# Dealing the first 512 rows of x to the first two row pairs in turn, in a fused QKV projection

## The chip, the cores and the metric

The kernel runs on one core of one Trainium2 chip. The metric is the device time of one execution in microseconds (us), as the median of several runs. Before the change it is 358.25 us, the median of 3 runs from 358.24 to 358.67 us.

TensorE (PE in the profile) multiplies, VectorE (DVE), ScalarE (ACT) and GpSimd (POOL) convert, add and copy, and SyncE (SP) issues most of the transfers between DRAM and the core's own memory. A transfer is carried by 16 DMA engines side by side.

## The reference

```python
def setup_inputs():
    batch, seq, hidden = 16, 512, 768
    return {
        "x": np.random.randn(batch, seq, hidden).astype(np.float32),
        "w_qkv": np.random.randn(hidden, 3 * hidden).astype(np.float32),
    }

def reference(x, w_qkv):
    qkv = np.matmul(x, w_qkv)
    q, k, v = qkv[..., :768], qkv[..., 768:1536], qkv[..., 1536:]
    return np.stack([q, k, v], axis=0).astype(np.float32)
```

It is one matrix product, 8192 x 768 by 768 x 2304, whose three column thirds are written as three separate arrays of 8192 x 768. Each row of the output depends on the same row of x alone, so which rows are worked on together is free, as long as a result is written back to the row that it came from.

## The kernel before, in words

The 8192 rows of x are worked on in 32 pairs of row tiles (`NP`), two tiles of 128 rows to a pair. The 2304 output columns are cut into two groups of 1024 (`Q_OFF`, the index `q`), each of two blocks of 512 (`CB`), and a remainder of 256 (`REM`). Pairs 2 to 31 multiply each group by a scheme of seven products for a 2 x 2 block product, which needs sums of blocks of x (`sums_x`) and of w (`sum_w`); products 1 and 2 are in bf16 and the others in f32r, and all go through line 245. Pairs 0 and 1 (`ND = 2`) are multiplied directly in bf16, in `block` (line 479), because the sums of w are not there yet. The remainder columns of every pair are multiplied directly in `rem` (line 308).

The order of the work is written out by hand (`manual_schedule`): each engine runs its instructions in the order in which the program issues them, and waits only for data or for a buffer. The transfers that SP issues are one ordered queue.

The start runs like this. SP first issues the loads of pair 0 and of pair 1 (`load_rows`, line 160), 768 KB each: partition m receives row m of the first tile and row m of the second, two pieces of 3072 bytes. Behind them in the same queue come the first weight block in six loads of 256 KB (`load_blocks(0, 0, 1)`, line 92), the second in two of 768 KB, the remainder's weights, and pair 2 in eight loads (`load_x_rows(2)`, line 137), which reads pieces of 768 bytes. Beside the loads TensorE multiplies zeros (`busy`, line 452). When pair 0 has landed, ACT and DVE convert it to bf16, each a share of the columns (`cast_row`, lines 165 and 166), TensorE turns it (`turn_row`, line 179), and DVE and ACT copy the turned tiles out of PSUM (`copy_row`, lines 186 and 188). Two more products of zeros follow, and then pair 1 goes the same way. After its twelve turns TensorE goes straight on to the products of the first weight block (line 479) and from there to the end of the program.

Results are stored by `store_quad` (two stores of 768 KB and 256 KB for each pair and column group, lines 298 to 303) and, for the remainder, by the last line of `rem` (line 323, 256 KB). For all pairs these take their place in DRAM from `rows_of`. Pairs 0 and 1 have eight stores of the first kind and two of the second. The remainder's staging tile has two buffers (`or_pool`), so the copy of pair 2's remainder out of PSUM (line 322) waits until the store of pair 0's has landed. The output tiles have five buffers (`o_pool`), and the input tiles three (`xin_pool`).

Pair 5 is loaded behind most of the stores of pairs 0 and 1 in SP's queue (`load_x(ND + 3, nc.sync)`, line 128); DVE then turns it (line 153), and POOL makes its sums (lines 212 to 216), which the seven products need.

Of the kernel before, what the change touches and what calls it, by code (L numbers as in the profile page):

```python
# [10 lines left out]
def kernel(  # L11
# [20 lines left out]
    nc = tc.nc  # L32
    P = 128
# [6 lines left out]
    KH = KT // 2  # L40
    KC = K // 4
    NP = M // (2 * P)
    CB = 512
    REM = N3 - 4 * CB
    Q_OFF = (0, 2 * CB + REM)
    R_OFF = 2 * CB
    fp32 = mybir.dt.float32
# [6 lines left out]
    x_flat = x.rearrange("b t h -> (b t) h")  # L54
    out_flat = out.rearrange("s b t h -> s (b t) h")
# [21 lines left out]

    b1 = [w_pool.tile([P, KT, CB], bf16, name=f"b1_{q}") for q in range(2)]
    b22 = [w_pool.tile([P, KH, CB], f32r, name=f"b22_{q}") for q in range(2)]
    t_0 = w_pool.tile([P, 4, KH, CB], f32r, name="t_0")  # L80
    w_rem[1] = rem_pool.tile([P, KH, REM], bf16, name="w_rem1")
# [39 lines left out]
    xin, xf, xb, sr = {}, {}, {}, {}  # L121
# [19 lines left out]
    def load_x(p, other):  # L141
        xin[p] = xin_pool.tile([P, 2 * P // G, KC], fp32, name="xin")
        load_x_half(p, 0, nc.sync)
        if other is not None:
            load_x_half(p, 1, other)

    def transpose(p, cuts=(0, 8)):
        if p not in xf:
            xf[p] = xf_pool.tile([P, KT, 2 * P], fp32, name="xf")
        turned = xf[p][:].rearrange("p j (g b) -> p g j b", b=G)  # L150
        rows = xin[p][:].rearrange("p g (a j) -> p g j a", a=G)
        for g, end in zip(cuts, cuts[1:]):
            nc.vector.transpose(turned[:, g:end], rows[:, g:end])  # L153

    def load_rows(p):
        xin[p] = xin_pool.tile([P, 2, K], fp32, name="xin")
        rows = x_flat[p * 2 * P:(p + 1) * 2 * P, :]
        nc.sync.dma_start(xin[p][:], rows.rearrange("(r m) k -> m r k", m=P))  # L160

    xc, turned_rows = {}, {}

# [63 lines left out]
    def quad(p, q, pool=o_pool, tag="o"):  # L227
        u = Quad()
        u.p, u.q = p, q
        u.o = pool.tile([P, 2, 2 * CB], fp32, name="o", tag=tag)  # L230
        u.x = u.y = u.z = None
        return u

    def product(u, n, ps, start):
        t1, t2, t3, t4 = ts[u.q]
        if n <= 2:
            h = (n - 1) * KH
            lhs = [xb[u.p][:, h + j, :P] for j in range(KH)]
            rhs = [b1[u.q][:, h + j, :] for j in range(KH)]
        else:  # L240
            k, t = {3: (4, b22[u.q][:]), 4: (0, t4), 5: (1, t1), 6: (2, t2), 7: (3, t3)}[n]
            lhs = [sr[u.p][:, k, j, :] for j in range(KH)]
            rhs = [t[:, j, :] for j in range(KH)]
        for j in range(KH):
            nc.tensor.matmul(  # L245
                ps[:], lhs[j], rhs[j],
                start=(start and j == 0), stop=(j == KH - 1), skip_group_check=True,
            )
# [7 lines left out]
    def do(u, n, out=True):  # L256
# [17 lines left out]
        elif n == 5:  # L274
            u.y = bank()
            product(u, 5, u.y, True)
            if u.p == NP - 1:
                nc.scalar.activation(c22, u.y[:], ident)
        elif n == 7:
            product(u, 7, u.x, False)  # L280
            if u.p == NP - 1:
                nc.vector.tensor_tensor(c22, c22, u.x[:], op=add)
# [8 lines left out]
            nc.vector.tensor_tensor(c12, c12, u.y[:], op=add)  # L291

    def rows_of(s, p, lo, hi):
        return out_flat[s, p * 2 * P:(p + 1) * 2 * P, lo:hi].rearrange("(r m) n -> m r n", m=P)

    def store_quad(u):
        if u.q == 0:
            nc.sync.dma_start(rows_of(0, u.p, 0, H), u.o[:, :, :H])
            nc.sync.dma_start(rows_of(1, u.p, 0, 2 * CB - H), u.o[:, :, H:])
        else:  # L300
            part = 2 * H - Q_OFF[1]
            nc.sync.dma_start(rows_of(1, u.p, H - part, H), u.o[:, :, :part])
            nc.sync.dma_start(rows_of(2, u.p, 0, H), u.o[:, :, part:])
# [9 lines left out]
    def rem(p, eng=nc.sync, between=None):  # L313
        ps = ps_pool.tile([P, 2, REM], fp32, name="ps")
        rem_row(p, 0, ps[:, 0, :])
        if between is not None:
            between()
        rem_row(p, 1, ps[:, 1, :])

        def copied():  # L320
            o = or_pool.tile([P, 2, REM], fp32, name="orem")
            act.activation(o[:], ps[:], ident)  # L322
            return lambda: eng.dma_start(rows_of(1, p, R_OFF - H, R_OFF - H + REM), o[:])

        return copied

    def two(a, b, early, u=None):

        do(a, 1)
        do(b, 1, u is None)  # L330
        if u is None:
            early()
            rem(a.p)()()
        else:
            middle(u)
            copied = rem(a.p, between=lambda: third(u))
            evacuate(b)
            early()
            copied()()
            fourth(u)  # L340
            load_x(a.p + 3, nc.sync)
        do(a, 2)
        do(b, 2)
        summed(a, b)
# [27 lines left out]
    def plain(a, b, c, d, early, rem_c, stored=False):  # L372

        add_first(a)
        add_first(b)
        rem(a.p)()()
        do(c, 1)
        do(d, 1)
        early()
        rem_c()  # L380
        do(c, 2)
        do(d, 2)
        add_second(a)
        add_second(b)
        if stored:
            for u in (c, d):
                store_cols(u, 0, 0, CB, nc.sync)
# [43 lines left out]
        rem_stored(a.p, 1, 2, lambda dst, src: act.activation(dst, src, ident), nc.sync)  # L431


    ND = 2
    zero = xb_pool.tile([P, CB], bf16, name="zero", tag="xb")
    nc.vector.memset(zero[:], 0.0)
    load_rows(0)
    nc.scalar.activation(tiny[:], zero[:, :1], ident)
    make_identity(nc, eye)
    load_rows(1)  # L440
    load_blocks(0, 0, 1)
    load_blocks(0, 1)
# [66 lines left out]
    def ahead(p, reversed_pair):  # L509
        transpose(p)  # L510
        if reversed_pair:
            sums_x(p)
            round_x(p)
        else:
            round_x(p)
            sums_x(p)
# [114 lines left out]
    def load_next(p, other):  # L631
        if p < NP:
            load_x(p, other)

    def early():
        ahead(ND + 2, False)
        load_x(ND + 3, nc.sync)

    two(quad(ND + 1, 0), quad(ND + 1, 1), early, u2)

    def early():
        ahead(ND + 3, True)
        load_x(ND + 5, nc.sync)

    two(quad(ND + 2, 0), quad(ND + 2, 1), early)
    transpose(ND + 4, (0, 4))

    for p in range(ND + 3, NP - 1, 2):
        first = p == ND + 3
# [6 lines left out]
        def early():  # L656
            ahead(p + 2, p + 2 < NP - 1)
            load_next(p + 4, nc.scalar)
# [6 lines left out]
        c, d = quad(p + 1, 0), quad(p + 1, 1)  # L665
        final = p + 3 >= NP
        plain(a, b, c, d, early, lambda: rem(c.p)()(), final)
# [32 lines left out]
```

## Time and profile before

| | before |
|---|---|
| median of 3 runs | 358.25 us (358.24 to 358.67) |
| the profiled execution's own time | 358.3 us |
| its span, first to last instruction | 356.5 us |
| TensorE busy | 351.5 us, 99% of the span |
| DVE, ACT, POOL busy | 264.3, 186.0, 177.3 us |
| read from DRAM, written to DRAM | 32.24 MB, 75.50 MB |
| granted TensorE clock, mean | 1.000 |

The profile is of one execution. The difference between its own time and its span, 1.8 us, lies before its first instruction and after its last. A page of the profile gives each engine's busy time, the transfers, and the chain of work that ended last, followed back from the last instruction. Beside it the trace can be asked for who waited for whom, for the chain in order of time, and for the busy time and the bytes moved in any stretch of the span. It also has a record of every packet that a DMA engine moved, with its start, its length in time and its size.

### The profile page before, as it was taken

The numbers are of one execution on the slowest core, as the hardware profiler recorded it, in microseconds if no ns is written. First come the engines' busy times: TensorE is split into PE (matmuls) and PEld (weight loads), VectorE is DVE, ScalarE is ACT, GpSimd is POOL, SyncE is SP. The second block draws the span as 40 slices with busy tenths as digits, with TensorE's granted clock in tenths as the row PEclk, the third lists the DMA queues.
The fourth block names the chain that finished last, engine by engine and source line by source line (L and its number), as shares of the span: only waits on it lengthen the run. The fifth ranks groups of instructions, "written<-read, shape, count | busy, mean of one in ns | idle before, by whom it ended". The sixth has DMA issues, their size and how long they took to land.

```text
span 356.5 us, 5348 instructions
## 1 busy us (share of the span) xinstructions
PE 351.5 (99%) x1782; PEld 252.2 (71%) x1782; DVE 264.3 (74%) x309; ACT 186.0 (52%) x321; POOL 177.3 (50%) x184
## 2 busy tenths in 40 slices
PE   7999999999999999999999999999999999999996
PEld 3474677768677686877768677686877868777675
DVE  3799876796877869777695876969777696876743
ACT  4587755445454553645545454553645545454553
POOL 0121773376566453665535566353665535566320
PEclk9999999999999999999999999999999999999999
DMA  7998999999999898998979889699999989887397
GB/s 297 379 351 258 323 373 344 371 325 360 293 337 311 250 362 204 357 258 299 351 189 385 229 311 338 174 406 242 346 272 299 331 196 390 232 295 293 146 377 273
DMA packets 82075, 108.10 MB, mean 303 GB/s; under 512 B 4992, under 2 KB 62080, under 8 KB 82048
## 3 DMA queue, kind: packets, MB, share of 16 engines
q1 hardware_dynamic: 75520, 103.04, 86.2%
q10 hardware_dynamic: 6528, 4.72, 5.1%
q8 instruction: 14, 0.23, 0.3%
q14 instruction: 13, 0.11, 0.1%
HBM read 32.24 MB, written 75.50 MB: 302 GB/s over the span
## 4 chain that ended last, share of the span: by engine, by line
PE 97%; DMA 2%; ACT 0%; SPq 0%; issue 0%
PE ps L245 79%; PE ps L308 11%; PE ps L479 6%; DMA xin<-in_x_dram 2%; PE ps L412 0%; PE ps L179 0%; ACT xc L166 0%; SPq L160 0%; ACT orem L431 0%
## 5 line engine op out<-in xcount | busy, mean ns | idle before, releaser
L245 PE MATMUL ps<-t,s 128*128 128x512 f32 x720 | 178.0, 395 | 0.0
L245 PEld LDWEIGHTS ps<-t,s 128*128 128x128 f32 x720 | 135.0, 188 | 29.6
L153 DVE STREAM_TRANSPOSE xf<-xin 128x768 f32<-128x768 f32 (+2 forms) x46 | 93.4, 2033 | 2.8 <-DMA xin<-in_x_dram 2.8
L245 PE MATMUL ps<-b,xb 128*128 128x512 bf16 x360 | 85.2, 379 | 0.0
L285 DVE TENSOR_TENSOR o<-o,ps 128x512 f32<-128x512 f32 x56 | 38.5, 687 | 51.8 <-ACT o L284 51.8
L192 POOL CAST xb<-xf 128x1536 bf16<-128x1536 f32 x28 | 41.0, 1465 | 56.9 <-DVE xf L153 56.9
L212 POOL TENSOR_TENSOR s<-xf 128x384 fp32r<-128x384 f32 x29 | 31.0, 1067 | 72.9 <-DVE xf L153 71.2
L245 PEld LDWEIGHTS <-xb 128*128 128x128 bf16 x360 | 34.0, 98 | 36.9 <-issue 4.2
L291 DVE TENSOR_TENSOR o<-o,ps 128x512 f32<-128x512 f32 x60 | 41.1, 686 | 20.7 <-PE ps L245 19.5
L284 ACT ACTIVATE o<-ps 128x512 f32<-128x512 f32 x56 | 33.5, 598 | 42.1 <-PE ps L245 42.1
L245 PE MATMUL ps<-b,s 128*128 128x512 f32 x180 | 50.6, 389 | 0.0
L288 ACT ACTIVATE o<-ps 128x512 f32<-128x512 f32 x60 | 35.9, 598 | 25.2 <-PE ps L245 22.8
L365 DVE TENSOR_TENSOR o<-o,ps 128x512 f32<-128x512 f32 x78 | 47.8, 681 | 0.0
L273 ACT ACTIVATE o<-ps 128x512 f32<-128x512 f32 x60 | 36.0, 599 | 19.1 <-PE ps L245 15.4
L308 PE MATMUL ps<-w_rem,xb 128*128 128x256 bf16 x372 | 45.7, 273 | 0.0
L322 ACT ACTIVATE orem<-ps 128x512 f32<-128x512 f32 x31 | 18.5, 597 | 49.1 <-PE ps L308 28.5
L308 PEld LDWEIGHTS <-xb 128*128 128x128 bf16 x372 | 36.2, 98 | 10.9 <-issue 0.3
L245 PEld LDWEIGHTS ps<-b,s 128*128 128x128 f32 x180 | 33.8, 188 | 7.0
L213 POOL TENSOR_TENSOR s<-s,xf 128x384 fp32r<-128x384 f32 x29 | 29.5, 1018 | 2.3
L214 POOL TENSOR_TENSOR s<-xf 128x384 fp32r<-128x384 f32 x29 | 29.4, 1015 | 0.0
L216 POOL TENSOR_TENSOR s<-xf,s 128x384 fp32r<-128x384 f32 x29 | 29.2, 1008 | 0.0
L369 ACT ACTIVATE o<-ps 128x512 f32<-128x512 f32 x26 | 15.5, 598 | 16.9 <-PE ps L245 16.1
(53 smaller groups left out, 164.9 us busy)
## 6 DMA issues: line engine op xcount, KB each, us to landing
out_dram<-o SPq DMA_DIRECT2D x60, 768.0 KB, 4.7
out_dram<-o SPq DMA_DIRECT2D x76, 256.0 KB, 3.9
xin<-in_x_dram SPq DMA_DIRECT2D x88, 192.0 KB, 5.6
out_dram<-orem SPq DMA_DIRECT2D x31, 256.0 KB, 2.4
xin<-in_x_dram ACTq DMA_DIRECT2D x24, 192.0 KB, 4.4
st<-in_w_qkv_dram SPq DMA_DIRECT2D x5, 768.0 KB, 7.7
xin<-in_x_dram SPq DMA_DIRECT2D x2, 768.0 KB, 4.9
st<-in_w_qkv_dram SPq DMA_DIRECT2D x6, 256.0 KB, 6.0
```

Of the source, the lines that this page charges most:

```text
L153: nc.vector.transpose(turned[:, g:end], rows[:, g:end])
L192: nc.gpsimd.tensor_copy(out=xb[p][:], in_=xf[p][:])
L212: 1: lambda g: g.tensor_tensor(s[:, 1], a21, a22, op=add),
L213: 2: lambda g: g.tensor_tensor(s[:, 2], s[:, 1], a11, op=sub),
L245: nc.tensor.matmul(ps[:], lhs[j], rhs[j], start=(start and j == 0), stop=(j == KH - 1), skip_group_check=True,)
L273: nc.scalar.activation(c12, u.x[:], ident)
L284: nc.scalar.activation(c22, u.x[:], ident)
L285: nc.vector.tensor_tensor(c22, c22, u.y[:], op=add)
L288: nc.scalar.activation(c21, u.x[:], ident)
L291: nc.vector.tensor_tensor(c12, c12, u.y[:], op=add)
L308: nc.tensor.matmul(ps, xb[p][:, j, r * P:(r + 1) * P], w_rem[j // KH][:, j % KH, :], start=(j == 0), stop=(j == KT - 1), skip_group_check= ...
L365: dve.tensor_tensor(c, c, u.z[:], op=add)
```

## The change

The two pairs that are multiplied directly, 0 and 1, take other rows than before. Pair 0 held rows 0 to 255 and pair 1 rows 256 to 511; now pair 0 holds the even and pair 1 the odd rows of the first 512. In each pair, partition m of tile r has row 256 r + 2 m + p instead of row 256 p + 128 r + m. The loads follow this and so do all stores of the two pairs, through `rows_of`. The pieces keep their size (3072 bytes in a load, 3072 or 1024 in a store) and their number. In DRAM two neighbouring partitions of one tile are 6144 bytes apart instead of 3072, and the two rows of one partition 786,432 bytes instead of 393,216. The second argument of `load_rows` has a default that leaves one transfer to a pair, and no call gives another. `ND` is only set earlier.

```diff
+    ND = 2
...
-    def load_rows(p):
+    def dealt(rows, p):
+        return rows[:ND * 2 * P].rearrange("(r m p) n -> p m r n", m=P, p=ND)[p]
+
+    def load_rows(p, tiles=2):
         xin[p] = xin_pool.tile([P, 2, K], fp32, name="xin")
-        rows = x_flat[p * 2 * P:(p + 1) * 2 * P, :]
-        nc.sync.dma_start(xin[p][:], rows.rearrange("(r m) k -> m r k", m=P))
+        for r in range(0, 2, tiles):
+            n = slice(r, r + tiles)
+            nc.sync.dma_start(xin[p][:, n], dealt(x_flat, p)[:, n])
...
     def rows_of(s, p, lo, hi):
+        if p < ND:
+            return dealt(out_flat[s, :, lo:hi], p)
         return out_flat[s, p * 2 * P:(p + 1) * 2 * P, lo:hi].rearrange("(r m) n -> m r n", m=P)
...
-    ND = 2
```

## The prediction

> **What bounds the kernel now.** I read the shares by engine first, then the chain that ended last, then the waits, and last the stretches of the span that the change touches. The table of stretches says how far TensorE leaves room (busy us and instructions of PE, PEld, DVE, ACT, POOL, then clock, DMA share, GB/s):
>
> ```profile
> 0.00:7.44 7.44, 5.39 (x24) 2.22 (x25) 1.82 (x6) 2.98 (x6) 0.70 (x6) 1.00 0.72 276
> 7.44:351.50 344.06, 344.06 (x1738) 248.49 (x1739) 261.36 (x302) 181.89 (x313) 176.63 (x178) 1.00 0.92 304
> ```
>
> From 7.44 to 351.50 us TensorE is never idle. So the end moves only in two ways: the moment 7.44 moves, or a hole opens in those 344 us. The chain in order of time says what sets 7.44:
>
> ```profile
> 0.74 0.44 SPq L160
> 1.24 5.62 DMA xin<-in_x_dram
> 6.88 0.45 ACT xc L166
> 7.44 0.85 PE ps L179 x12
> 8.29 0.86 PE ps L479 x4
> ```
>
> The landing of pair 1's rows at 6.86 starts the conversion, the conversion starts the turns, and after these TensorE does not stop. A microsecond on this landing is a microsecond on the end. Pair 0 is ahead in the same queue, so what matters is when 1.57 MB (two times 768 KB) have arrived. The rate of the transfers by stretch:
>
> ```profile
> 1.90:2.40 0.50, 0.50 (x2) 0.15 (x1) 0.00 (x0) 0.32 (x2) 0.00 (x0) 1.00 0.54 104
> 2.40:2.90 0.50, 0.50 (x3) 0.18 (x2) 0.00 (x0) 0.00 (x0) 0.00 (x0) 1.00 0.79 258
> 2.90:3.40 0.50, 0.50 (x3) 0.23 (x2) 0.00 (x0) 0.00 (x0) 0.00 (x0) 1.00 1.04 424
> 3.40:6.40 3.00, 2.59 (x19) 1.25 (x17) 0.84 (x3) 0.94 (x2) 0.00 (x0) 1.00 1.02 413
> ```
>
> ```profile
> 6.90:10.80 3.90, 3.45 (x26) 1.92 (x26) 3.02 (x9) 3.30 (x9) 0.00 (x0) 1.00 1.05 405
> ```
>
> ```profile
> 17.00:18.00 1.00, 1.00 (x6) 0.46 (x5) 1.00 (x2) 0.21 (x1) 1.00 (x2) 1.00 1.12 241
> ```
>
> ```profile
> 34.00:38.00 4.00, 4.00 (x20) 1.78 (x19) 4.00 (x4) 4.00 (x9) 0.36 (x1) 1.00 1.04 411
> ```
>
> The loads of pairs 0 and 1 ramp up for one microsecond and then run at 413 to 424 GB/s. The packet records show the same: the first one or two packets of 3072 bytes on an engine take 119 to 576 ns, and from 3.0 us to the end of both loads nearly every one takes 121 ns. The last engine's part of pair 1 lands at 6.86, the first one's at 6.34.
>
> **The change part by part.**
>
> *Instructions.* Nothing is added, removed or moved on any engine or queue: two loads and ten stores get other DRAM addresses, with pieces of the same size and number. The moved `ND` and the loop in `load_rows` issue what was issued before: one transfer to a pair. This costs 0, and needs no cover.
>
> *The steady part of the two loads.* It runs at 413 to 424 GB/s with the rows of a tile 3072 bytes apart. The weight loads from 6.90 to 10.80 read 2048-byte pieces that lie 55,296 bytes apart (six rows of w to a partition), nine times the new distance, at 405 GB/s. Both ends of the distance scale run within 5% of each other, and packet times of 121 ns without scatter say that each DMA engine moves at its own pace, not at DRAM's. Lower end: at 424 instead of 413 the steady 3.9 us would shorten by 0.1. Upper end: the slowest stretch of loads in the trace, 241 GB/s at 17 to 18 us, where pair 2 is read in 768-byte pieces from 96 KB of DRAM; 1.57 MB would take 6.5 us there instead of 3.8, 2.7 more. The weight loads are the nearer row, since their pieces are long and spread out as the new ones are. I take 0 and keep -0.1 and +2.7.
>
> *The ramp of the two loads.* From 1.90 to 2.90 us the transfers moved 0.5 x (104 + 258) = 181 KB; at 413 GB/s they would have moved 413. The missing 232 KB are 0.56 us. If the slow first packets come from engines that meet in the same part of DRAM, larger distances could shorten this; if they come from opening more places, they would lengthen it. The trace has another ramp, when the next weight block is read after pair 2 (18.5 to 20 us): there the pieces lie far apart, and single first packets still take 540 to 741 ns. So distance alone does not remove slow first packets, though 768-byte loads are in flight beside them. Lower end: the whole 0.56 us go; if also the spread in the engines' first packets (1.92 to 2.51 us) went, 32 packets of 118 ns each from 1.92 and the 0.30 us from the last packet's end to its landing would give 5.98, 0.88 earlier. Upper end: the ramp doubles, +0.56. I take 0.
>
> *What moves with the landing.* Everything behind the two loads in SP's queue shifts with them, since the engines work the queue off in order: the weight rows land from 7.50 on, and TensorE's start shifts by the same time. So the head is carried over one to one.
>
> *The ten stores.* They carry 4 x 768 + 4 x 256 + 2 x 256 KB = 4.7 MB between 28 and 54 us, and two waits hang on them:
>
> ```profile
> ACT orem L322 <- DMA out_dram<-orem: 1.9, 1, 1.9
> DVE xf L153 <- DMA xin<-in_x_dram: 2.4, 1, 2.4
> ```
>
> The first is the copy of pair 2's remainder, which waits until 31.96 for the store of pair 0's remainder. Behind it on ACT stand the last three conversions of a weight block (line 457), which end at 34.60; TensorE started that block at 32.40 and wants the third of them after 14 products of 0.22 us, at 35.5. The cover is 0.9 us. The second is pair 5's turn, which waits until 56.36 for its load behind the stores; POOL's second sum of it ends at 61.65, and TensorE asks for it at 63.86. The cover is 2.2 us. Bounds: the stores of both shapes ran at 411 GB/s from 34 to 38 us, paced by the engines (121 ns and 46 ns a packet), so a gain buys nothing, TensorE having no hole there to close: 0. At the slow end, 241 instead of 411 GB/s, 4.7 MB would take 19.5 us instead of 11.4, 8 more, of which 5.9 would be left over the cover of 2.2. I take 0, because the stores that are there now include 1024-byte pieces 3072 bytes apart as well as whole rows, and both run at the engines' pace.
>
> *Sum.* 0 + 0 + 0 against the profiled execution's 358.3 us (356.5 span and 1.8 around it). The median of the runs is 358.25, 0.05 below it, so I predict 358.25 us: no change. A difference of less than 0.2%, 0.72 us, is about what a measurement of this kernel can't tell from no change.
>
> **A rule against this change.** The row first: the trace reads at 413 GB/s with 3072 bytes between partitions and at 405 GB/s with 55,296. The Trainium skill, "DMA: Bandwidth & Descriptors", section "Latency and other measured facts", reports that copies slow down when the rows of the partitions lie at large powers of two apart: 207 GB/s at 512 KiB, 164 at 2 MiB, 103 at 4 MiB. Here the distances become 6 KiB between partitions and 768 KiB between a partition's two rows, three times a power of two. By the page's figures I estimate at most a fall as from 207 to 164, to 0.79 of the rate, which would make the 3.8 us of the loads 1.0 longer; by the rows it is 0. No run here has yet shown a rate at these distances.
>
> **The rivals.**
>
> *The ramp gets shorter.* For it: the first packets take up to 576 ns against 121, and the next ones do not. Against it: the other ramp, over far places, has longer ones. Removing 0.28 to 0.56 us gives 357.7 to 358.0; the extreme of 0.88 us gives 357.4. Even that is cut: TensorE's ten products of zeros run until 5.2, and turning pair 0 and two more products of zeros need 1.4 us after that, so pair 1's turns can't begin before 6.6, 0.8 before 7.44. Only the last part of this case is past 0.72 us.
>
> *The loads get slower (the other side).* The place is the landing of pair 1. The mechanism: even rows and then odd rows open every place of the region twice, and sixteen engines at twice the distance meet more often in one part of DRAM, so that packets are longer than 121 ns. Against it are the weight loads. A doubled ramp gives 358.8; 241 GB/s throughout gives 361.0. By how much it decides: packets of 144 ns instead of 121 (32 of them on an engine, 0.72 us).
>
> *The stores get slower.* They must cost over 0.9 us before 31.9, or 2.2 by 56, before TensorE sees it; a tenth on 11.4 us is hidden, and at 25% more the 0.65 us beyond cover give 358.9. The full slow end gives 364.
>
> *The change doesn't do what it says* in that the distance does not matter to an engine-paced load: that is my forecast.
>
> **How the numbers follow.** No change within 0.3 us (358.0 to 358.6): 0.58. Ramp shorter: 0.18, of which 0.08 beyond 0.72 us, with the scatter of the runs (0.43 us from lowest to highest) taken in. Loads slower: 0.17, of which 0.12 beyond; 0.05 of the 0.17 is for distances at which the engines fall on the same part of DRAM throughout, with up to 2.7 us. Stores slower: 0.07, of which 0.06 beyond. So faster 0.08, slower 0.18, the same 0.74. The range from 357.7 to 359.1 leaves out the 0.08 below and about 0.1 of the slow cases above: it takes in the ramp's 0.56 both ways and not the far ends of 241 GB/s.
>
> **What the profile after would show.** If I am right: 121 ns for the packets of both loads after 3 us, pair 1 landing between 6.6 and 7.1, the turns at 7.2 to 7.7, no hole in TensorE from there to its last product. If the ramp is shorter, the stretch from 1.90 to 2.90 moves clearly over 181 KB, and 7.44 comes earlier by as much as the time falls. If the loads are slower, the stretch from 3.40 to 6.40 falls under 400 GB/s. If the stores are, ACT's wait at line 322 ends well after 31.96 less the shift of the head, or TensorE has idle time after 35 or 63 us. I am wrong if the ramp depends strongly on where the first packets read, or if a small shift lets one DMA engine fall behind at another place: between 30.50 and 33.00 the transfers ran at 81 GB/s while the last engine's packets were awaited.

## The result: slower by 0.13%

The changed kernel takes 358.76 us (median of 22 runs, 358.66 to 359.37), the kernel before 358.32 us beside it (22 runs, 358.24 to 358.76). The ratio is 1.0013 with a 95% interval of 1.0007 to 1.0019: 0.44 us between the medians. The profiled execution took 358.74 us, its span is 357.0 us (356.5 before).

The chain in order of time of the changed kernel (start, length in us, what) has the same members as before, and one of them is longer (the last row ends with the window at 9 us):

```profile
0.74 0.44 SPq L165
1.23 6.08 DMA xin<-in_x_dram
7.33 0.45 ACT xc L171
7.88 0.85 PE ps L184 x12
8.73 0.43 PE ps L485 x2
```

Pair 1 lands at 7.31 instead of 6.86 us, and its turns start at 7.88 instead of 7.44. That is 0.44 to 0.45 us, all of the difference. The stretches of the span (the last column is GB/s) say which part of the two loads it is (a packet counts in the stretch in which it starts):

```profile
1.90:2.40 0.50, 0.50 (x2) 0.15 (x1) 0.00 (x0) 0.32 (x2) 0.00 (x0) 1.00 1.72 123
2.40:2.90 0.50, 0.50 (x3) 0.18 (x2) 0.00 (x0) 0.00 (x0) 0.00 (x0) 1.00 0.10 18
2.90:3.40 0.50, 0.50 (x3) 0.23 (x2) 0.00 (x0) 0.00 (x0) 0.00 (x0) 1.00 0.82 332
3.40:6.40 3.00, 1.97 (x13) 0.80 (x11) 0.63 (x2) 0.94 (x2) 0.00 (x0) 1.00 1.02 410
```

From 3.40 us on the rate is 410 GB/s against 413. Before that, 123, 18 and 332 GB/s stand against 104, 258 and 424: over 1.5 us that is 0.5 x (104 + 258 + 424 - 123 - 18 - 332) = 157 KB less, which at 413 GB/s are 0.38 us. The packet records show which packets are long. Below are the start and length in ns of the first twelve packets of 3072 bytes, in order of their start (the records have no engine number):

```
before:  (1920,  576) (1946,  174) (2026,  522) (2027,  513) (2059,  373) (2113,  127)
         (2146,  212) (2151,  119) (2162,  119) (2162,  255) (2164,  248) (2170,  267)
after:   (1840,  119) (1859,  122) (1914, 1074) (2001,  998) (2061,  904) (2067,  956)
         (2112,  851) (2126,  698) (2129,  651) (2178,  173) (2201,  173) (2205,  559)
```

Sixteen packets now take 0.56 to 1.07 us, where before a single one does (0.58 us). All sixteen are in flight together from 2.37 to 2.76 us, and there are never more than 16 at once, apart from overlaps of a few ns: one on each engine, its first or its second. After them nearly every packet takes 121 ns as before. Summed over the 512 packets of both loads, the time over 121 ns is 0.22 us an engine before and 0.77 after. The landing moved by less than these 0.55 us of difference because it follows the engine that ends last: the last packet ends at 7.00 us, against 6.56 before.

Behind the head no new wait came up: from 9 us to the last products, the list of TensorE's waits has no row, before and after. The two waits that hang on the stores are both shorter:

```profile
ACT orem L329 <- DMA out_dram<-orem: 1.4, 1, 1.4
DVE xf L154 <- DMA xin<-in_x_dram: 0.9, 1, 0.9
```

The first was 1.9 before and the second 2.4. The store of pair 0's remainder lands at 31.86 us as against 31.87, though it was issued 0.5 us later.

### The profile page after: what moved, and what is told of

Same layout as the page of the kernel before. It is cut to its first block, busy times and chain, and to the rows that moved or that the text cites. A ratio compares the mean times of both kernels' runs of the same rounds, so it can differ in the third digit from the quotient of the medians.

```text
span 357.0 us, 5329 instructions
## 1 busy us (share of the span) xinstructions
PE 350.0 (98%) x1763; PEld 252.2 (71%) x1782; DVE 263.5 (74%) x309; ACT 186.2 (52%) x321; POOL 177.7 (50%) x184
## 4 chain that ended last, share of the span: by engine, by line
PE 74%; POOL 15%; DVE 6%; issue 3%; DMA 2%; ACT 0%; SPq 0%
PE ps L250 56%; PE ps L315 11%; PE ps L485 6%; DVE xf L154 6%; POOL xb L197 5%; POOL s L218 3%; POOL s L217 3%; POOL s L219 3%; DMA xin<-in_x_dram 2%; PE ps L419 0%; PE ps L184 0%; DVE o L296 0%; ACT xc L171 0%; SPq L165 0%; ACT orem L438 0%
## 5 line engine op out<-in xcount | busy, mean ns | idle before, releaser
L250 PE MATMUL ps<-b,xb 128*128 128x512 bf16 x343 | 81.4, 379 | 1.1
L329 ACT ACTIVATE orem<-ps 128x512 f32<-128x512 f32 x31 | 18.5, 597 | 48.2 <-PE ps L315 30.5
```

What stands on the lines that cost most here:

```text
L250: nc.tensor.matmul(ps[:], lhs[j], rhs[j], start=(start and j == 0), stop=(j == KH - 1), skip_group_check=True,)
```

## The experiments

The theories at the start: the two loads alone cost the time, or the stores take part in it; and if it is the loads, the distance between neighbouring partitions, the distance between a partition's two rows, or the number of separate places that the first packets touch makes them long.

**Loads alone and stores alone.** In `e1_loads_only` `rows_of` loses its two new lines; in `e2_stores_only` `load_rows` reads as before.

```diff
 e1:
-        if p < ND:
-            return dealt(out_flat[s, :, lo:hi], p)
 e2:
-            nc.sync.dma_start(xin[p][:, n], dealt(x_flat, p)[:, n])
+            rows = x_flat[p * 2 * P:(p + 1) * 2 * P, :].rearrange("(r m) k -> m r k", m=P)
+            nc.sync.dma_start(xin[p][:, n], rows[:, n])
```

> Only the two loads take the even and odd rows; the ten stores write to the places of before, so the rows of the first 512 come out permuted. If the loads are the whole cause: pair 1 lands near 7.3 us as in the changed kernel, the turns start near 7.9, and the time is 0.45 us over before. If the stores are the cause: pair 1 lands near 6.9 and the time is that of before.

> Only the ten stores write to even and odd rows; the loads read as before, so the rows of the first 512 come out permuted. If the loads are the whole cause: pair 1 lands near 6.9 us and the time is within 0.1 us of before. If the stores cost anything: over 0.2 us more than before with the head unchanged, and a hole in TensorE's work after 30 us.

With the loads alone: 358.77 us against 358.53 of before, 1.0009 (1.0000 to 1.0018); the runs of before spread more here (358.27 to 359.31), and between the fastest runs of each lie 0.35 us. Pair 1 lands at 7.16 and the excess over 121 ns is 0.72 us an engine. With the stores alone: 358.50 us, 0.9999 (0.9990 to 1.0008), pair 1 at 6.76, an excess of 0.20. The loads carry the loss and the stores none that can be measured. The ramp itself varies from one execution to another: the old layout landed at 6.86 and 6.76 us here, the new one at 7.31 and 7.16.

**One distance at a time.** `e3_tiles_interleaved` keeps the old distance between partitions and takes the new one between a partition's rows. `e4_adjacent_rows` does it the other way about, with the two rows next to each other. `e9_partitions_apart` takes the new distance between partitions with the old one between the rows.

```diff
-        return rows[:ND * 2 * P].rearrange("(r m p) n -> p m r n", m=P, p=ND)[p]
 e3:
+        return rows[:ND * 2 * P].rearrange("(r p m) n -> p m r n", m=P, p=ND)[p]
 e4:
+        return rows[:ND * 2 * P].rearrange("(p m r) n -> p m r n", m=P, p=ND)[p]
 e9, in load_rows of the kernel before:
+        first = x_flat[p * 1:p * 1 + 1, :]
+        rows = bass.AP(first.tensor, first.offset, [[2 * K, P], [128 * K, 2], [1, K]])
+        nc.sync.dma_start(xin[p][:], rows)
```

> Pair p takes rows 128 p + m and 256 + 128 p + m: neighbouring partitions 3072 bytes apart as before, the two rows of a partition 786,432 bytes apart as in the changed kernel. Loads and stores agree. If the long first packets come from the distance between neighbouring partitions: pair 1 lands near 6.9 us, time as before. If they come from the distance between a partition's two rows: it lands near 7.3, 0.45 us slower.

> Pair p takes rows 256 p + 2 m + r: neighbouring partitions 6144 bytes apart as in the changed kernel, the two rows of a partition next to each other, so that a pair is one stretch of DRAM again and a partition reads 6144 bytes in one stretch. If the distance between neighbouring partitions is the cause: pair 1 lands near 7.3 us, 0.45 us slower. If the number of separate places that the first packets touch is the cause (half as many stretches as before, each twice as long): near 6.9, time as before or up to 0.3 us faster. If the distance between a partition's two rows is the cause: near 6.6, up to 0.3 us faster.

> Partition m of pair p reads rows 2 m + p and 2 m + p + 128: neighbouring partitions 6144 bytes apart as in the changed kernel, a partition's two rows 393,216 bytes apart as before. Rows 128 to 383 are read twice and others not, so the first 512 rows of the output are not the reference's. If the distance between partitions alone costs the 0.45 us: pair 1 lands near 7.3 us and the time is 0.45 over before. If the cost needs both distances (the span of the reads doubled): near 7.0, at most 0.2 us over before.

| | partitions apart, rows | a partition's rows apart | GB/s, 1.90 to 3.40 us | pair 1 lands, us | median, us | before beside it | ratio (95%) |
|---|---|---|---|---|---|---|---|
| before | 1 | 128 | 262 | 6.86 | 358.32 | | |
| e3 | 1 | 256 | 172 | 7.18 | 358.46 | 358.53 | 0.9999 (0.9990 to 1.0007) |
| e9 | 2 | 128 | 201 | 7.08 | 358.55 | 358.33 | 1.0006 (0.9996 to 1.0015) |
| e4 | 2 | 1 | 311 | 7.05 | 358.59 | 358.53 | 1.0005 (0.9996 to 1.0014) |
| after | 2 | 256 | 158 | 7.31 | 358.76 | 358.32 | 1.0013 (1.0007 to 1.0019) |

Neither distance alone makes a loss that the times can tell from none; but the intervals of e9 and e4 reach past 1.0013 too, so for these two they can't tell it from the full loss either. In the profiles each of the three lands between before and after, by 0.19 to 0.32 us late. The profiled execution of e3 took 358.62 us, one of the two slowest of its runs, so its 7.18 is rather a late one.

e4 must be read with care, because its pieces differ: each partition's two rows move as one packet of 6144 bytes, 256 packets in all, most of them of 234 ns. Its ramp is faster than before, and what makes it late is the stretch behind:

```profile
1.90:3.40 1.50, 1.50 (x5) 0.56 (x4) 0.00 (x0) 0.32 (x2) 0.00 (x0) 1.00 0.88 311
3.40:6.40 3.00, 2.82 (x15) 1.07 (x14) 0.63 (x3) 0.94 (x2) 0.00 (x0) 1.00 1.00 394
```

So e4 shows that the new distance between partitions does not slow the ramp when a partition's rows move as one packet, and its landing tests nothing more. The other profiles do not single out one distance: in this stretch the old layout ran at 262 GB/s here and at 240 and 295 in e13 and e2, the new one at 158 and at 188 in e1, and e9 and e3 lie lower than the old one with one new distance each. The slow ramp of e3's profile is not in the median of its runs, 358.46 us, against 358.77 for the new loads (e1) on the same chip. What share each distance has stays open, and so does the number of places: e3 has as many as before and a slow ramp, e4 half as many and a fast one.

**In a running stream.** A weight load of 256 KB is put ahead of both loads, in the kernel before (e5) and in the changed one (e6), so that the loads of x no longer meet the start of the transfers.

```diff
+    first_w = tq_pool.tile([P, KT, CB], fp32, name="st0", tag="tq")
+    load_w(first_w[:, 0:1], 0, 1, Q_OFF[0], CB)
     load_rows(0)
...
     load_rows(1)
-    load_blocks(0, 0, 1)
+    for j in range(1, KT):
+        load_w(first_w[:, j:j + 1], j, 1, Q_OFF[0], CB)
+    stage[0, 0, 0], stage[0, 1, 0] = first_w[:, :KH, :], first_w[:, KH:, :]
```

> The kernel before with one weight load of 256 KB put ahead of the two loads of x, so that it meets the start of the transfers; the loads of x then follow in a running stream. It is the base for the next run. Pair 1 lands 0.6 us later than in the kernel before (256 KB at 413 GB/s) plus or minus the change in the ramp, near 7.5 us, and the time is 0.3 to 1.0 us over before.

> The changed kernel with the same weight load ahead. If the distances cost only in the first packets after an idle start: all packets of 3072 bytes take about 121 ns, pair 1 lands within 0.1 us of the run before, and so does the time. If the distances slow the loads wherever they stand: pair 1 lands 0.4 us later than in the run before, and the time is 0.4 us over it.

In e5 pair 1 lands at 7.36 and the time is 358.83 us. In e6 it lands at 8.00, 0.64 later, and the time is 360.19 us (four runs from 359.07 to 360.51; the profiled one is the slowest). The stretches of e5 first and then of e6, as above:

```profile
2.90:3.40 0.50, 0.50 (x3) 0.23 (x2) 0.00 (x0) 0.00 (x0) 0.00 (x0) 1.00 1.01 361
3.40:3.90 0.50, 0.50 (x3) 0.20 (x2) 0.00 (x0) 0.00 (x0) 0.00 (x0) 1.00 1.02 412
```

```profile
2.90:3.40 0.50, 0.50 (x3) 0.22 (x2) 0.00 (x0) 0.00 (x0) 0.00 (x0) 1.00 1.38 248
3.40:3.90 0.50, 0.50 (x3) 0.20 (x2) 0.00 (x0) 0.00 (x0) 0.00 (x0) 1.00 0.59 190
```

The hole is there again, just where the packets of x begin. So it does not come from the start of the transfers: the excess of the packets of x is 0.07 us an engine in e5 and 0.57 in e6. The rest of the loss in e6's profiled execution lies on TensorE, as told further down. How much of the 0.64 us every run of e6 has is open, since its fastest is only 0.24 us over e5's median.

**All partitions at one place, and far apart.** `e8_same_rows` lets all partitions of a pair read the same two rows. `e7_wide` and `e11_three_rows` take larger distances.

```diff
-        rows = x_flat[p * 2 * P:(p + 1) * 2 * P, :]
-        nc.sync.dma_start(xin[p][:], rows.rearrange("(r m) k -> m r k", m=P))
+        first = x_flat[p * 1:p * 1 + 1, :]
+        rows = bass.AP(first.tensor, first.offset, [[D * K, P], [R * K, 2], [1, K]])
+        nc.sync.dma_start(xin[p][:], rows)
 D and R stand for numbers:
 e8: D = 0, R = 2     e7: D = 16, R = 8     e11: D = 3, R = 384
```

> All 128 partitions of pair p read the same two rows, p and p + 2, instead of their own, so the first 512 rows of the output are not the reference's; everything else as in the kernel before. If the first packets wait for each separate place of DRAM to be opened: the shortest ramp, pair 1 lands near 6.5 us, up to 0.4 us faster than before. If they wait because the engines meet at one place: the longest ramp and a lower rate all through, pair 1 lands after 7.3 us.

> Partition m of pair p reads rows 16 m + 8 r + p: neighbouring partitions 49,152 bytes apart, a partition's two rows 24,576 bytes apart, the whole over 2048 rows. The first 512 rows of the output are not the reference's. If the cost grows with the span that the first packets cover (6.3 MB instead of 1.6): pair 1 lands later than in the changed kernel, after 7.5 us, over 0.6 us slower than before. If it comes from certain distances at which the engines, still in step, meet: anything between 6.8 and 7.4, with no order by distance.

> Partition m of pair p reads rows 3 m + 384 r + p: distances half as large again as in the changed kernel, 9216 and 1,179,648 bytes. The first 512 rows of the output are not the reference's. If the cost grows with the span: pair 1 lands near 7.5 us, 0.6 us slower than before. If it comes from the distances being three times a larger power of two, at which the engines meet: near 6.9 us, time as before.

In e8 the first packets end at 2.3 to 2.5 us, much as before (2.1 to 2.5), but then the rate is low for 2.5 us while all engines read the same two rows; after that it recovers in part:

```profile
2.90:5.40 2.50, 2.50 (x7) 0.72 (x5) 0.00 (x0) 0.00 (x0) 0.00 (x0) 1.00 0.64 176
5.40:9.40 4.00, 1.62 (x15) 0.87 (x14) 0.98 (x3) 0.94 (x2) 0.00 (x0) 0.97 1.00 338
```

Pair 1 lands at 9.91 and the time is 363.35 us. Of the 5.0 us over before, 3.05 are the landing; in the profiled execution, of 364.01 us, most of the rest is a slower TensorE, whose granted clock (the third column from the right) falls by half from 9.17 to 16.0 us, in the second of two waits of 1.8 us:

```profile
9.20:15.90 6.70, 5.41 (x22) 2.80 (x23) 3.39 (x11) 3.44 (x10) 0.00 (x0) 0.50 1.05 404
```

e7 lands at 7.63 and takes 360.23 us; of its 1.87 us over the kernel before beside it, 0.77 are the landing and 0.7 are waits of TensorE behind it, twice for weights and once without a releaser; the last 0.4 was not traced. Not all of its landing is the ramp: SP needs 0.66 and 0.59 us for the two issues instead of 0.44 and 0.45, and the first packet starts at 2.19 instead of 1.92. e11, with distances half as large again as in the changed kernel, lands at 7.23 and takes 358.71 us, 1.0011 (1.0002 to 1.0020). A cost that grows with the span would have given 7.5, one from certain multiples of a power of two 6.9. Neither is borne out: away from the old layout it is late, by about the same amount for two rows and for three.

**One tile at a time, and the second tiles exchanged.** `e10_split_tiles` cuts each load of the kernel before in two. `e12_swapped_second_tile` exchanges the second tiles of the two pairs.

```diff
 e10:
-        nc.sync.dma_start(xin[p][:], rows.rearrange("(r m) k -> m r k", m=P))
+        for r in range(2):
+            nc.sync.dma_start(xin[p][:, r], rows[r * P:(r + 1) * P, :])
 e12:
-        return rows[:ND * 2 * P].rearrange("(r m p) n -> p m r n", m=P, p=ND)[p]
+        first = rows[p:p + 1]
+        step = 2 * P + 1 if p == 0 else 2 * P - 1
+        return bass.AP(first.tensor, first.offset, [[ND * H, P], [step * H, 2], [1, rows.shape[1]]])
```

> The kernel before with each of the two loads of x cut into one transfer per tile, so that the first packets of all engines read from one tile (two stretches of 96 KB instead of four) and the second tile follows. If the cost grows with the number of places that the first packets touch: a shorter ramp, pair 1 lands near 6.7 us, 0.1 to 0.2 us faster than before. If it depends on certain distances alone: within 0.1 us of before.

> The changed kernel with the two pairs' second tiles exchanged: pair 0 takes the even rows of the first 256 and the odd rows of the second 256, pair 1 the others. The step between a partition's two rows becomes 257 or 255 rows instead of 256, all else stays. If the cost grows with the span: no difference to the changed kernel, pair 1 near 7.3 us, 0.45 us slower than before. If it comes from the exact step of 256 rows, at which the first and second packet meet: near 6.9 to 7.1, at most 0.2 us slower than before.

e10 was to be the better version and is worse: 359.43 us, 1.0036 (1.0022 to 1.0049). Its ramp is short (233, 350 and 399 GB/s), and pair 0 lands at 4.84 us, 0.17 earlier than before. Then the rate breaks down while pair 1 is read, with single packets of up to 0.99 us, and pair 1 lands at 7.96, 1.10 later than before:

```profile
3.40:4.40 1.00, 1.00 (x4) 0.35 (x3) 0.36 (x1) 0.52 (x1) 0.00 (x0) 1.00 1.04 347
4.40:6.40 2.00, 2.00 (x17) 1.09 (x15) 0.71 (x2) 0.52 (x1) 0.00 (x0) 1.00 0.79 221
```

Reading from a single tile is not enough to explain it, because pair 0 is read in the same way. Why pair 1's loads break down is open.

e12 lands at 7.23, like the changed kernel and not like the one before, so the exact step of 256 rows is not needed for the loss. Its time, 365.47 us, says nothing about the loads: SP holds stores of the two pairs back for each other, presumably because in this form they count as overlapping:

```profile
SPq L332 <- DMA out_dram<-orem: 8.6, 1, 8.6
```

**Another place, and a place read before.** With the earlier runs it was open whether the layout or the place in DRAM makes the packets long, and whether the first reading does. e13 and e14 take both loads 4096 rows further down, in the old and in the new layout. e15 reads a part of every fourth of the 512 rows first, 256 KB or a sixth of the bytes.

```diff
 e13, in the kernel before:
-        rows = x_flat[p * 2 * P:(p + 1) * 2 * P, :]
+        rows = x_flat[M // 2 + p * 2 * P:M // 2 + (p + 1) * 2 * P, :]
 e14, in the changed one:
-            nc.sync.dma_start(xin[p][:, n], dealt(x_flat, p)[:, n])
+            nc.sync.dma_start(xin[p][:, n], dealt(x_flat[M // 2:], p)[:, n])
 e15, in the changed one:
+    touched = x_flat[:4 * P, :CB].rearrange("(m q) k -> m q k", q=4)
+    nc.sync.dma_start(both[:, 1, :CB], touched[:, 0])
     load_rows(0)
```

> The kernel before, with the two loads taken 4096 rows further down in x (12.6 MB), in the old layout; the first 512 rows of the output are not the reference's. If the layout makes the first packets long: pair 1 lands near 6.9 us and the time is within 0.15 us of before. If the place in DRAM does: it can land anywhere from 6.6 to 7.4.

> The changed kernel with the two loads 4096 rows further down in x, in the new layout; the first 512 rows of the output are not the reference's. If the layout makes the first packets long: pair 1 lands 0.3 to 0.5 us later than in the run before, near 7.3. If the place in DRAM does: no fixed difference to the run before.

> The changed kernel with a load of 256 KB ahead, as with the weight load ahead of both, but from x itself: 2048 bytes of every fourth of the first 512 rows, into a tile that is not read. If the first packets wait because a place of DRAM is read for the first time: the loads of x follow without long packets and pair 1 lands near 7.4 us, as with the weight load ahead of the old layout. If they wait because of the distances themselves, whatever was read before: near 8.0, as with the weight load ahead of the new layout.

The stretches of e13 and then of e14:

```profile
1.90:2.40 0.50, 0.50 (x2) 0.15 (x1) 0.00 (x0) 0.32 (x2) 0.00 (x0) 1.00 0.35 74
2.40:2.90 0.50, 0.50 (x3) 0.18 (x2) 0.00 (x0) 0.00 (x0) 0.00 (x0) 1.00 0.71 227
2.90:3.40 0.50, 0.50 (x3) 0.22 (x2) 0.00 (x0) 0.00 (x0) 0.00 (x0) 1.00 1.03 418
```

```profile
1.90:2.40 0.50, 0.50 (x2) 0.15 (x1) 0.00 (x0) 0.32 (x2) 0.00 (x0) 1.00 1.89 98
2.40:2.90 0.50, 0.50 (x3) 0.18 (x2) 0.00 (x0) 0.00 (x0) 0.00 (x0) 1.00 0.13 31
2.90:3.40 0.50, 0.50 (x3) 0.23 (x2) 0.00 (x0) 0.00 (x0) 0.00 (x0) 1.00 0.70 283
```

The old layout at the other place is as fast as before: pair 1 at 6.87 us, 358.36 us, 1.0002 (0.9992 to 1.0011). The new one shows the hole again, deeper: pair 1 at 7.72, 359.69 us, 1.0039 (1.0024 to 1.0054); 0.4 us of this is a later wait of TensorE for a converted tile of x. So it is the layout; in this one profile the place adds to its size. In e15 a sixth of the bytes had been read before, and the hole stays, with an excess of 0.42 us an engine:

```profile
2.90:3.40 0.50, 0.50 (x3) 0.22 (x2) 0.00 (x0) 0.00 (x0) 0.00 (x0) 1.00 0.79 213
3.40:3.90 0.50, 0.50 (x3) 0.20 (x2) 0.00 (x0) 0.00 (x0) 0.00 (x0) 1.00 0.93 338
```

Pair 1 lands at 7.74, midway between the 7.4 and the 8.0 that the two theories gave, and the time is 360.41 us, 1.0060 (1.0045 to 1.0075); TensorE is slower here as in e6. So this run does not decide whether the first reading takes part.

## Why the prediction was wrong

I forecast no change, 358.25 us, and the kernel became slower by 0.44 us, clear of the runs' scatter though smaller than the 0.72 us that I had taken as the least that can be told. By the prediction's own steps:

- *Where a change can act.* Right. The 0.45 us on pair 1's landing came out as 0.44 us at the turns and 0.44 us in the median.
- *Instructions.* Right: the same order on every engine, and no new wait on TensorE from 9 us to the last products.
- *The steady part of the loads.* Right: 410 GB/s against 413, and packets of 121 ns. The power-of-two rule that I set against the change (the Trainium skill, "DMA: Bandwidth & Descriptors", section "Latency and other measured facts") describes a lower rate; at these distances no lower rate is seen in the steady part.
- *The ramp of the loads.* This is the step that failed. I had put its slow end at 0.56 us, a doubled ramp, and took 0. It measured 0.44 to 0.45 us, four fifths of that end. The mechanism was named, in the rival of slower loads (engines that meet more often, packets longer than 121 ns), and its price for a doubled ramp, 358.8 us, is close to the 358.76 measured. But I gave the rival 0.17, of which 0.12 went to losses beyond 0.72 us, and set its threshold by longer packets throughout (144 ns on 32 of them), while it acts on one or two packets of each engine. What misled me was the row that I took for the choice: the slow first packets of the weight load at 18.5 to 20 us. I read them as "distance alone does not remove slow first packets" and concluded that distance does not matter. They stood beside 768-byte loads, at another distance and another size, and could say nothing about what a doubling does. The range from 357.7 to 359.1 holds the measured time because it takes in the ramp's 0.56 us both ways; the term in the sum was wrong all the same. The weight loads from 6.90 us were evidence for the steady rate alone.
- *The stores.* Right: 0.9999 (0.9990 to 1.0008) with the stores changed alone. The cover of 0.9 us was not touched.

What stays open is the cause inside DRAM or the engines. Shown is that the hole belongs to the new layout at both places, that it comes at the first packets of x wherever these stand in the stream, that it is still there when a sixth of the bytes was read before, that the distance between partitions alone does not bring it when a partition's rows move as one packet (e4), and that the size of the lateness does not follow the distance (two rows, three rows and the exchanged tiles land within 0.15 us of each other). Not shown is what share each of the two distances has. That engines which start in step meet at one part of DRAM until they have fallen out of step would agree with the hole, and with the low rate of e8; it is an explanation that was only argued, and e10, where pair 0 loads fast and pair 1 does not, shows that it is not the whole account.

No layout that was tried loads the two pairs faster than that of the kernel before.

## What to carry to other kernels

A load's steady rate says nothing about its first packets; where a load is first on the path to the first product, price its ramp for itself, and when the only bounds are "gone" and "doubled", do not take the middle as if it had been measured. The ramp can be measured cheaply by putting both layouts behind another load and at another place: a hole that moves with the layout belongs to the layout. A wider spread of addresses is no gain by itself: the two new distances cost 0.44 us together, and either of them alone gained nothing that could be measured. And when an experiment changes a layout, count the packets: in e4 the pieces had become twice as long, and the rate behind the ramp was another, 394 against 413 GB/s.

## What the runs showed of the hardware that I had not expected

- Splitting a transfer of two tiles into one transfer per tile slowed the second pair: 221 GB/s from 4.40 to 6.40 us, where the kernel before has 413 from 3.40 to 6.40, for the same rows and pieces (e10). The first pair landed 0.17 us earlier. The order in which pieces are read can matter, though what in it does is open.
- Reading the same two rows from all engines ran at 176 GB/s from 2.90 to 5.40 us and at 338 from 5.40 to 9.40, with packets of 121 ns still the commonest, 272 of 512 (e8).
- A clock of 1.00 in a profile's row can mean that nothing is recorded there. In the kernel before, the products of zeros start 0.43 us apart until 4.62 us and the products from then on 0.22; the trace's first clock record, at 1.00, begins at 4.62 us, and the rows ahead of it print 1.00 too, as the mean of 1.000 counts them as full. In e6 that record begins only at 10.54 us, and in e15 at 10.17. Until then the turns start 107 ns apart instead of 56, and so the first twelve take 1.48 us instead of 0.95:

```profile
6.03 0.95 PE L179 MATMUL ps<-eye,xc 128*128 128x128 bf16 x12 [0.48 <-ACT xc L166]
6.69 1.48 PE L184 MATMUL ps<-eye,xc 128*128 128x128 bf16 x12 [1.06 <-ACT xc L171]
```

  The first row is of e5, the second of e6. This is what makes e6 slower than its landing explains: its products on the first weight block start 1.48 us later than in e5 and the first takes 0.21 us longer, 1.69 of the 1.71 us between the two profiled executions, and 0.64 of it is the landing. In e6 and e15 TensorE's wait for pair 0, of 1.06 and 0.82 us, began before the record; in e7, where a wait of 0.91 us left the turns at 0.95, the record begins at 5.10 us, ahead of the wait. What puts the record off was not tried.
